# Seven of layer 1's eight MLP sets from seven block products, and GpSimd's taps of the second half from the first half's second product on, thirteen a block

## The chip, the cores and the metric

The kernel runs on one core of a Trainium2 chip. The metric is the device time of one execution in microseconds (us). The core has TensorE (PE, matrix products; PEld is its weight load), VectorE (DVE), ScalarE (ACT), GpSimd (POOL) and SyncE (SP, which issues most transfers). Each takes its instructions in program order from its own queue, and waits on semaphores for what another engine or a transfer has to deliver.

## The reference

1024 tokens of width 1024 pass two layers, all in float32. Layer 0 mixes tokens by a gated linear recurrence (HGRN2), layer 1 by a causal convolution; behind each stands an MLP with 4096 hidden columns and a squared ReLU, and each sum with the residual is normalised.

```python
u = h @ w_pw1 + b_pw1
a, gate = split(u, 2)
u = a * sigmoid(gate)
u = depthwise_conv(u, w_dw) + b_dw          # 31 taps, causal, each channel by itself
u = silu(layer_norm(u, ln_g, ln_b))
mix = u @ w_pw2 + b_pw2
x = layer_norm(ALPHA * x + mix, ...)
ff = square(relu(x @ ffn_w1[1])) @ ffn_w2[1]
x = layer_norm(ALPHA * x + ff, ...)
```

The change touches layer 1 from the convolution to the end of the MLP's first product.

## The kernel before

**Products.** Every float32 operand is cut into a high part (a cast on ScalarE) and a low part (a subtraction on VectorE, here called a cut), and a product is three matmuls: high by high, high by low, low by high. A matmul is 128 by 128 weights against 512 columns.

**Halves, blocks, sets.** The tokens are two halves of 512. The convolution's channels are eight blocks of 128. The MLP's 4096 hidden columns are eight sets of 512. A set can be done in two ways. Classical: eight products of 128 x 1024 by 1024 x 512, four for each half of the tokens (`UA`, first half; `UB`, second half), 96 matmuls a half. Or by the seven block products of a Strassen scheme (24 matmuls each, 168 in all): weights and tokens are cut into 2 x 2 blocks, sums of blocks (the forms) are multiplied, and sums of the seven results give the set. Products 1 and 2 need the first half of the tokens alone (`E`, function `soon`); products 3, 6, 5, 7 and 4 need the second half too (`L`, class `LateUp`). In the program's names `xa` and `xc` hold the tokens in high and low parts, and later forms of them; `xf` holds form 6; `s` is the scratch in which VectorE adds up a form; `wa` are weights for `UA`, `UB` and `E`; `raw`, `sum` and `fw` are weight blocks, their sums and their cut forms for `L` (class `LateForms`: four sums and five cuts for a set). `NEAR` is the number of sets done classically.

**The order of the stages** is the string `SEQ`. `P0j`, `P1j` are the pointwise products of channel block j for the two halves, `N` the normalisation of a half's convolution, `F` its activation, `S` the second pointwise product with the residual's normalisation, then `UA`, `E`, `UB`, `L` as above.

**The convolution** runs beside TensorE. The last `NPOOL[half]` of the 31 taps of a block go to GpSimd: ScalarE multiplies a tap (`prod`, L1555), GpSimd adds it to the sum `cb` (`cb<-cb,prod`; the first tap is written to `cb` directly, so 11 taps are 10 adds). The other taps are multiplied and added by VectorE in a PSUM bank (`ps<-u,par,ps`), the first by ScalarE (L1567). VectorE adds both, TensorE transposes the block (`ident,cb`), and ScalarE copies it (L1583) for `N`.

**What sets the order around the change.** A planner in the program (class `Background`) keeps clocks for TensorE, VectorE and GpSimd by costs of its own and places taps between the matmuls; `bg.hold` keeps GpSimd's taps back. Where a stage begins, `gate` ties the first tap to a tile of that stage: a one-element copy (L1550) that GpSimd has to make first. `bg.chores` are pieces of side work (the turning of normalised tokens, the forms) that are placed one by one between products; `bg.done()` places all that are left. The whole is then put in order once more by the framework's scheduler, which simulates a timeline and fixes each engine's queue before the program is built.

**S.** `second` normalises four tiles of 128 tokens, t = 0 to 3. VectorE makes mean and variance, GpSimd raises the variance to the power -1/2 (`mv<-mv,nhalf`, L518), ScalarE applies both (L1693), TensorE transposes (`ident,y`), ScalarE scales while it copies (L1667) and casts (L435), VectorE cuts.

**The forms of the second half** (`late_forms`): for two halves k of a block, the chores `fifth`, `sixth`, `fourth`, and, once nothing reads the plain tokens any more, `sevenths` and `last_form`, which write into `xc`.

**The loads of the MLP's second product** (`dh<-hf`) read tiles that `up_half` and `LateUp.form` have stored in device memory (`hf`, L1184). `ahead` lists weights that layer 0's free slots cut beforehand and store as `ready` (`spare`, L1398); there are 38 such tiles.

Of the kernel before, what the change touches and what calls it, by code (L numbers as in the profile page):

```python
# [17 lines left out]
S = 1024  # L18
KB = D // P
# [3 lines left out]
TAPS = 31  # L23
PAD = TAPS - 1
NFC = 8
NEAR = 2
ALPHA = 4.0 ** 0.25
LN_EPS = 1e-5
RMS_EPS = 1e-6
# [6 lines left out]

KBYTES = 220
PAIRS = [("q", 0), ("q", 1), ("q", 2), ("q", 3), ("g", 0), ("q", 4), ("q", 5), ("q", 6), ("g", 1), ("q", 7), ("g", 2), ("g", 3)]
NPOOL = (12, 11)
SEQ = "P00 P01 P02 P03 P04 P05 P06 P07 P10 P11 P12 P13 N0 P14 F0 P15 S0 P16 P17 UA0 UA1 E2 E3 N1 E4 F1 E5 E6 S1 E7 UB0 UB1 L2 L3 L4 L5 L6 L7"  # L40

# [225 lines left out]
def body(ctx, tc, d, out):  # L269
# [21 lines left out]
    def ring(kbs, shape, name, dt=F32):  # L291
        return Ring([view(kb, shape, dt, name) for kb in kbs])

    def run(kb, n, size):
        return [kb + i * size for i in range(n)]

    def slots(kbs, name):
        return ring(kbs, (2, 1024), name, F32R)

    def raws(kbs, name="raw"):  # L300
        return ring(kbs, (1024,), name)

    def bank(ids):
        return Ring([banks[:, i] for i in ids])

    class Room:


        def __init__(self, parts, want):
            self.rings = {}  # L310
            parts = [list(p) for p in parts]
            for name, (shape, n, *dt) in sorted(want.items(), key=lambda w: -prod(w[1][0])):
                kb, at = (prod(shape) + 7) // 8 / 32, []
                for _ in range(n):
                    part = next(p for p in parts if p[1] - p[0] >= kb)
                    at.append(part[0])
                    part[0] += kb
                self.rings[name] = ring(at, shape, name, *dt)
# [4 lines left out]
    bg = Background()  # L323
# [177 lines left out]
    for k in range(4):  # L501
        c = slice((k % 2) * HT, (k % 2 + 1) * HT)
# [608 lines left out]
    ha = [dram.tile([P, 2048], F32, name=f"ha{c}") for c in range(NFC)]  # L1111

    ready = {}
    ahead = [("wpw1", (j, i)) for j in range(KB) for i in (1, 0)] + [("wpw2", (n, k)) for n in range(2) for k in range(4)] + [("w1", (i,)) for i in range(4 * NEAR)] + [("w1q", (1, c, i)) for c in range(NEAR, NEAR + 3) for i in range(2)]

    def blocks(name, layer, c):
        return [d[name][layer, c, q] for q in range(4)]
# [133 lines left out]
    class LateUp(Up):  # L1251


        def __init__(self, xs):
            self.layer, self.xf, self.turned = 1, xs, NEAR
            self.zs, self.ws = bank((1, 5, 2, 6)), bank((3, 7, 0, 4))
            self.c = ring((132, 134, 136, 138, 128, 130), wide_t, "c")
            self.hr = ring((0, 8, 16, 24) if NEAR % 2 == 0 else (16, 24, 0, 8), (2, 2, HT), "hr")
            self.t = ring(run(112, 4, 2), (2, 256), "ht")
# [12 lines left out]
        def begin(self, c):  # L1272

            u = self.of[c]
            for q in range(2):
                u["z", q] = self.zs()
                nc.scalar.copy(out=u["z", q], in_=u["p"][:, q])
# [46 lines left out]
    def plan_down(layer, fw, fh):  # L1324
        fw.plan([form("w2", layer, c, i) for i in ORDER for c in range(NFC)])
        fh.plan([hf[layer][c][i] for i in ORDER for c in range(NFC)])
# [158 lines left out]
    wa = Slots(nc, vector, slots([192, 200, 208, 96, 104, 176], "wa"), raws(run(20, 3, 4)))  # L1485
    steps = [(w[:-1], int(w[-1])) for w in SEQ.split()]

# [27 lines left out]
    def pointwise(half, j):  # L1515
        wG, wA = wa.take(2)
        pg, pa = acc(), acc()
        product(pg, narrow(wG, x2T[half]))
        product(pa, narrow(wA, x2T[half]))
        wa.ahead(3)  # L1520
        if len(conv) >= 6:
            bg.flush(conv[-6])
        sg = big("r")
        nc.scalar.activation(sg, pg, AF.Sigmoid, bias=par[:, BPW1 + KB + j : BPW1 + KB + j + 1])
        u = big("u")
        if half == 0:
            nc.gpsimd.memset(u[:, :PAD], 0.0)
        else:
            nc.scalar.copy(out=u[:, :PAD], in_=halo[:, j, :])
        vector.scalar_tensor_tensor(out=u[:, PAD:], in0=pa, scalar=par[:, BPW1 + j : BPW1 + j + 1], in1=sg, op0=ALU.add, op1=ALU.mult)  # L1530
        if half == 0:
            nc.scalar.copy(out=halo[:, j, :], in_=u[:, HT:])
        sums = {}
        pooled.append(convolve_pool(half, j, u, sums))
        conv.append(convolve(half, j, u, sums, pooled[-1]))
        bg.pooled.append(pooled[-1])
        bg.jobs.append(conv[-1])

    def tap(j, i):
        return par[:, TAP + j * TAPS + i : TAP + j * TAPS + i + 1]  # L1540

    def convolve_pool(half, j, u, sums):
# [5 lines left out]
        if gate[0] is not None:  # L1548

            nc.gpsimd.tensor_copy(out=cb[:, :1], in_=gate[0])  # L1550
            gate[0] = None
        for k in range(TAPS - NPOOL[half], TAPS):
            first = k == TAPS - NPOOL[half]
            tp = cb if first else big("prod")
# [5 lines left out]
    def convolve(half, j, u, sums, other):  # L1560
# [6 lines left out]
        nc.scalar.activation(ca, u[:, :HT], AF.Identity, bias=par[:, BDW + j : BDW + j + 1], scale=tap(j, 0))  # L1567
        for i in range(1, TAPS - NPOOL[half]):
            if i == 6:
# [45 lines left out]
    def residual_of(half, y):  # L1615
        for t in range(NTB):
            nc.sync.dma_start(out=y[:, t, :], in_=kept[half][t])
        rest[half] = y
# [133 lines left out]
    for op, i in steps:  # L1752

        if op + str(i) in ("P10", "S0", "S1", "UA0", "UB0"):
            bg.done()

        bg.hold = op in ("N", "F", "S") or bg.hold and op == "P1"
        if op == "S":
            gate[:2] = sT[i][:, 1, KB - 1, :1].bitcast(F32), [ct[i][:, NTB - 1, :1]] * 2
            wa.behind = [gate[0]] * (3 if i == 0 else 0)  # L1760
        bg.margin = 12.0 if op == "S" else 5.0 if op in ("N", "F") else 0.0 if op != "P1" else bg.margin
        if op in ("P0", "P1"):
            pointwise(int(op[1]), i)
        elif op == "N":
            normalise(i)
        elif op == "F":
            finish(i)
        elif op == "S":
            second(i)
        elif op == "UA":  # L1770
            if i == 0:
                residual_of(1, view(32, (NTB, D), F32, "y"))
                for of in to_sum:
                    block_sums(*of, x3T[0][:2, 1, KB - 1, HT - 1 :].bitcast(F32), adds=adds)
            up_half(1, i, 0, wa, stA, x3T[0])
        elif op == "E":
            soon(i, wa, stA, {1: x3T[0][:, :, :4], 2: x3T[0][:, :, 4:]})
        elif op == "UB":
            if i == 0:
                wa.raws = None  # L1780
                wa.slots = slots((192, 200, 208, 96), "wa")
                stB = {"hr": ring(run(0, 2, 16), (8, 2, 256), "hb"), "r": ring(run(128, 2, 2), wide_t, "r"), "t": ring(run(112, 4, 4), (2, 2, 256), "ht")}
                xs, sevenths, last_form = late_forms()
            if i == NEAR - 1:
                bg.done()
                lf = LateForms(nc, vector, slots((104, 200, 208, 96, 192), "fw"), raws((176, 180, 184, 188)), raws((44,), "sum"))
                lf.todo = [[(blocks("w1q", 1, c),)] for c in range(NEAR, NFC)]
                lf.ahead(1)

                up = LateUp(xs)  # L1790
                up.bring(NEAR)

                def begin():
                    up.begin(NEAR)
                    for seventh in sevenths:
                        seventh()
                    last_form()

                up_half(1, i, 1, wa, stB, x3T[1], (lambda: None, lambda: lf.ahead(2), lambda: lf.ahead(3), begin))
            else:  # L1800
                up_half(1, i, 1, wa, stB, x3T[1])
        else:
            if i > NEAR:
                up.begin(i)
            if i < NFC - 1:
                up.bring(i + 1)
            for k in LATER if i > NEAR else (3, 6, 5, 7, 4):
                (f,) = lf.take(1)
                lf.ahead(3)
                up.form(i, k, f)  # L1810
                if i == NFC - 1 and k == 6:
                    fw = Slots(nc, vector, slots([48, 104, 200, 208, 144, 152, 160], "dw"), raws([40, 176, 180, 44, 140, 136], "dr"))
                    fh = Slots(nc, vector, slots([56, 32, 0, 8, 64, 72, 80], "dh"))
                    plan_down(1, fw, fh)
                if i == NFC - 1 and k in (6, 5):
                    fw.ahead(1 if k == 6 else 2)
                    fh.ahead(1 if k == 6 else 2)
# [106 lines left out]
```

## Time and profile before

| What | Value |
| --- | --- |
| Time, median of 3 runs | 2060.35 us (2057.59 to 2062.96) |
| Span of the profiled execution | 2068.3 us |
| TensorE busy | 2031.0 us, 98% |
| VectorE, ScalarE, GpSimd busy | 72%, 53%, 19% |
| Granted TensorE clock | 1.00 from 1301 to 1643 us |
| Product `S`, first half | 1306.8 to 1354 us |
| `P16`, `P17` | 1354 to 1379.8 us |
| `UA0` to `E6` with `N1`, `F1` | 1379.8 to 1483 us |
| `S`, second half | 1483 to 1531 us |
| `E7`, then `UB0`, `UB1` | 1531 to 1545, 1545 to 1588.7 us |
| `L2` to `L7` | from 1588.7 us |

The profiled execution is 8 us longer than the median of the runs; times on its axis are used for differences. A row of the timeline reads: start, duration, engine, line of the program, operation, what it writes and from what, shape, count; in brackets the idle time of the engine before it and what ended that. A row of the windows view reads: stretch, its length, then for each engine its busy time and its number of instructions, the granted clock, the transfers' share and rate.

### The profile page before, as it was taken

How to read it: one execution, taken by the hardware profiler on the slowest of the kernel's cores; microseconds unless marked ns; L12 is line 12 of the kernel's file. 1: busy time of each engine (PE TensorE's matmuls, PEld its weight loads, DVE VectorE, ACT ScalarE, POOL GpSimd, SP SyncE). 2: the span in 40 equal slices, each digit the busy share in tenths (PEclk: the TensorE clock that was granted, in tenths of full speed). 3: DMA queues.
4: the chain of work that ended last, by engine and by line, in shares of the span. 5: the costliest groups of instructions: out<-in, count | busy, mean ns of one | idle time of the engine just before them, and what ended most of it. 6: DMA issues, size and time to landing. Idle time of an engine off the chain costs nothing. (4 is left out here: it accounts for less than half of the span.)

```text
span 2068.3 us, 29719 instructions
## 1 busy us (share of the span) xinstructions
PE 2031.0 (98%) x11192; PEld 1674.5 (81%) x11192; DVE 1482.9 (72%) x1976; ACT 1090.2 (53%) x1727; POOL 388.4 (19%) x387
## 2 busy tenths in 40 slices
PE   8999999999999999999999999999999999999998
PEld 7888777788888888888888888888878878888886
DVE  8698877877775666565567898889589666755556
ACT  5456555641464555444444776488625555343333
POOL 0112222111001000000001699079210000100002
PEclk9999999999999999999999999999999999999999
DMA  4778889852689786999998855587759778996542
GB/s 186 224 195 233 238 224 270 254 189 81 187 288 298 243 295 221 353 341 332 335 349 292 309 193 185 190 323 271 256 215 339 245 232 291 386 292 204 193 155 102
DMA packets 183944, 517.55 MB, mean 250 GB/s; under 512 B 17912, under 2 KB 49784, under 8 KB 182776
## 3 DMA queue, kind: packets, MB, share of 16 engines
q1 hardware_dynamic: 168312, 456.93, 62.6%
q0 software_dynamic: 15488, 58.72, 12.3%
q8 instruction: 87, 1.43, 0.3%
q14 instruction: 57, 0.47, 0.1%
HBM read 380.85 MB, written 201.85 MB: 282 GB/s over the span
## 5 line engine op out<-in xcount | busy, mean ns | idle before, releaser
L204 PE MATMUL ps<-dw,dh 128*128 128x512 f32 x2688 | 611.6, 389 | 1.9 <-ACT dh L72 1.1
L204 PEld LDWEIGHTS ps<-dw,dh 128*128 128x128 f32 x2688 | 504.1, 188 | 107.2 <-ACT dh L72 1.6
L204 PE MATMUL ps<-x1f,fw 128*128 128x512 f32 x1344 | 309.3, 390 | 2.3 <-DVE c L204 1.2
L204 PEld LDWEIGHTS ps<-x1f,fw 128*128 128x128 f32 x1344 | 251.1, 188 | 56.2 <-ACT c L1224 2.3
L204 PE MATMUL ps<-xf,fs 128*128 128x512 f32 x1008 | 249.3, 398 | 4.1 <-issue 1.9
L204 POOL TENSOR_TENSOR cb<-cb,prod 128x512 f32<-128x512 f32 x168 | 222.7, 1334 | 12.9 <-ACT prod L1555 2.3
L204 DVE TENSOR_TENSOR dh<-dh 128x1024 fp32r<-128x1024 f32 x112 | 136.4, 1222 | 117.3 <-ACT dh L72 117.1
L204 PEld LDWEIGHTS ps<-xf,fs 128*128 128x128 f32 x1008 | 184.5, 189 | 43.4 <-issue 2.1
L204 DVE SCALAR_TENSOR_TENSOR ps<-u,par,ps 128x512 f32<-128x512 f32 x296 | 206.2, 750 | 11.0 <-ACT ps L1567 9.5
L72 ACT CAST dh<-dh 128x1024 fp32r<-128x1024 f32 x112 | 117.4, 1051 | 163.7 <-DMA dh<-hf 163.7
L204 PE MATMUL ps<-xa,wa 128*128 128x512 f32 x864 | 203.1, 392 | 0.1
L204 PEld LDWEIGHTS ps<-xa,wa 128*128 128x128 f32 x864 | 160.3, 188 | 33.3 <-ACT ha L1289 0.3
L204 DVE TENSOR_TENSOR dw<-dr,dw 128x1024 fp32r<-128x1024 f32 x112 | 136.2, 1222 | 66.6 <-ACT dw L72 65.9
L72 ACT CAST dw<-dr 128x1024 fp32r<-128x1024 f32 x112 | 117.0, 1051 | 119.2 <-PE ps L204 100.2
L1555 ACT ACTIVATE prod<-u,par 128x512 f32<-128x512 f32 x168 | 119.8, 726 | 36.6 <-POOL cb L204 35.7
L518 POOL TENSOR_TENSOR mv<-mv,nhalf 128x1 f32<-128x1 f32 x32 | 43.3, 1355 | 407.6 <-DVE mv L204 407.6
L1408 POOL COPY next<-ss 128x1 f32<-128x1 f32 x38 | 21.2, 558 | 413.8 <-DVE spare L204 265.1
L204 PE MATMUL ps<-xb,wa 128*128 128x512 f32 x384 | 91.1, 393 | 0.0
L204 PE MATMUL ps<-w,oT 128*128 128x512 f32 x384 | 89.5, 391 | 1.3 <-ACT oT L932 0.8
L204 DVE TENSOR_TENSOR spare<-next,spare 128x1024 fp32r<-128x1024 f32 x38 | 46.5, 1224 | 60.6 <-ACT spare L1401 60.5
L204 PE MATMUL ps<-vw,xf 128*128 128x512 f32 x336 | 79.8, 399 | 6.0 <-ACT vw L435 5.2
L204 PEld LDWEIGHTS ps<-w,oT 128*128 128x128 f32 x384 | 71.5, 188 | 16.6 <-ACT oT L932 1.2
(236 smaller groups left out, 2959.6 us busy)
## 6 DMA issues: line engine op xcount, KB each, us to landing
wa<-ready SPq DMA_DIRECT2D x140, 512.0 KB, 5.5
dh<-hf SPq DMA_DIRECT2D x112, 512.0 KB, 5.3
sum_w<-in_w_dram POOLq DMA_DIRECT2D x40, 1024.0 KB, 10.9
ready<-spare SPq DMA_DIRECT2D x76, 512.0 KB, 4.6
raw<-in_w1q_dram SPq DMA_DIRECT2D x66, 512.0 KB, 4.4
dr<-sum_w SPq DMA_DIRECT2D x64, 512.0 KB, 5.7
hf<-ht SPq DMA_DIRECT2D x112, 256.0 KB, 4.9
dr<-in_w_dram SPq DMA_DIRECT2D x48, 512.0 KB, 5.3
```

The source lines that it names most:

```text
L72: self.nc.scalar.copy(out=slot[:, 0, c], in_=raw[:, c])
L204: return op(*args, **kw)
L518: nc.gpsimd.tensor_tensor(out=dst, in0=src, in1=nhalf[:, :n], op=ALU.pow)
L1408: nc.gpsimd.tensor_copy(out=raw[:, :1], in_=now)
L1555: nc.scalar.activation(tp, u[:, k : k + HT], AF.Copy, scale=tap(j, k))
```

## The change

- `NEAR` goes from 2 to 1: set 1 is no longer `UA1` and `UB1`, but `E1` (products 1 and 2) and `L1` (3, 6, 5, 7, 4), seven block products.
- `NPOOL` goes from (12, 11) to (12, 13): GpSimd takes two more taps of each block in the second half, and VectorE two fewer.
- `bg.hold` no longer covers `S`: GpSimd's taps of the second half may start in the first half's `S`.
- `ahead` holds the same number of tiles: four classical weights fewer, and the block weights of two more sets.
- `bg.done()`, which places the remaining chores, moves from ahead of the last `UB` to its last product, since the last `UB` is now also the first.

```diff
-NEAR = 2
+NEAR = 1
-NPOOL = (12, 11)
-SEQ = "... S0 P16 P17 UA0 UA1 E2 E3 N1 E4 F1 E5 E6 S1 E7 UB0 UB1 L2 L3 L4 L5 L6 L7"
+NPOOL = (12, 13)
+SEQ = "... S0 P16 P17 UA0 E1 E2 E3 N1 E4 F1 E5 E6 S1 E7 UB0 L1 L2 L3 L4 L5 L6 L7"
-    ahead = ... + [("w1", (i,)) for i in range(4 * NEAR)] + [("w1q", (1, c, i)) for c in range(NEAR, NEAR + 3) for i in range(2)]
+    ahead = ... + [("w1", (i,)) for i in range(4 * NEAR)] + [("w1q", (1, c, i)) for c in range(NEAR, NEAR + 5) for i in range(2)]
     for op, i in steps:
         if op + str(i) in ("P10", "S0", "S1", "UA0", "UB0"):
             bg.done()
-        bg.hold = op in ("N", "F", "S") or bg.hold and op == "P1"
+        bg.hold = op in ("N", "F") or bg.hold and op == "P1"
...
             if i == NEAR - 1:
-                bg.done()
                 lf = LateForms(...)
                 lf.todo = [[(blocks("w1q", 1, c),)] for c in range(NEAR, NFC)]
                 lf.ahead(1)
                 up = LateUp(xs)
                 up.bring(NEAR)
                 def begin():
+                    bg.done()
                     up.begin(NEAR)
                     for seventh in sevenths:
                         seventh()
                     last_form()
```

What this does to the engines' queues is shown at three places. First GpSimd, from the end of the first half's taps (`mv<-mv,nhalf 128x4` is `N0`) through `S0` to `N1`; the single-column `mv` are `S0`'s roots.

```order
-L204 TENSOR_TENSOR cb<-cb,prod 128x512 x2
+L204 TENSOR_TENSOR cb<-cb,prod 128x512 x14
 L518 TENSOR_TENSOR mv<-mv,nhalf 128x1
-L204 TENSOR_TENSOR cb<-cb,prod 128x512 x68
+L204 TENSOR_TENSOR cb<-cb,prod 128x512 x4
+L518 TENSOR_TENSOR mv<-mv,nhalf 128x1
+L204 TENSOR_TENSOR cb<-cb,prod 128x512 x3
+L518 TENSOR_TENSOR mv<-mv,nhalf 128x1
+L204 TENSOR_TENSOR cb<-cb,prod 128x512 x3
+L518 TENSOR_TENSOR mv<-mv,nhalf 128x1
+L204 TENSOR_TENSOR cb<-cb,prod 128x512
+L86 COPY raw<-xa 128x1 x2
```

Before, three of `S0`'s four roots came first of all, then two adds, the fourth root and 68 adds. Now 14 adds stand ahead of the first root (the row that stays, L518), and the other three roots stand among the adds; 59 more adds follow, 84 in all.

Second, TensorE from the last products of the pointwise stage (`xb,wa`, to the end of `P17`) into `UA0` (`xa,wa`). Before:

```order
L204 MATMUL ps<-xb,wa 128x512 x9
L204 MATMUL ps<-ident,y 128x128 x4
L204 MATMUL ps<-xb,wa 128x512 x23
L204 MATMUL ps<-ident,y 128x128 x4
L204 MATMUL ps<-xb,wa 128x512 x5
L204 MATMUL ps<-ident,cb 128x128 x4
L204 MATMUL ps<-xb,wa 128x512 x5
L204 MATMUL ps<-xa,wa 128x512 x70
```

And now:

```order
L204 MATMUL ps<-xb,wa 128x512 x33
L204 MATMUL ps<-ident,y 128x128 x4
L204 MATMUL ps<-xb,wa 128x512 x2
L204 MATMUL ps<-ident,y 128x128 x4
L204 MATMUL ps<-xb,wa 128x512 x30
L204 MATMUL ps<-ident,y 128x128 x8
L204 MATMUL ps<-ident,cb 128x128 x8
L204 MATMUL ps<-xa,wa 128x512 x67
```

The transposes of the last token tile stood 33 and 10 matmuls ahead of `UA0`'s first; now all eight stand right ahead of it, and eight transposes of convolution blocks with them.

Third, the start of the `L` sets. TensorE's queue now, from `UB0` (`xc,wa`) on:

```order
L204 MATMUL ps<-xc,wa 128x512 x22
L204 MATMUL ps<-xc,fw 128x512 x8
L204 MATMUL ps<-xf_12586,fw 128x512 x6
L204 MATMUL ps<-xa,fw 128x512 x6
L204 MATMUL ps<-xf_12586,fw 128x512 x6
L204 MATMUL ps<-xa,fw 128x512 x18
L204 MATMUL ps<-xf_12586,fw 128x512 x36
L204 MATMUL ps<-xa,fw 128x512 x24
L204 MATMUL ps<-xc,fw 128x512 x48
```

Ahead of these rows `UB0` and product 3 of set 1 are mixed; 120 matmuls lie before the first that reads `xf`, where there were 216. The last row holds product 3 of set 2 and then product 7 of set 1. In the same stretch VectorE's queue, where form 7 is cut into `xc`:

```order
L204 TENSOR_TENSOR s<-xc 128x1024
L204 TENSOR_TENSOR xc<-s,xc 128x1024
L204 TENSOR_TENSOR s<-s,xc 128x1024
L204 TENSOR_TENSOR dh<-dh 128x1024
L204 TENSOR_TENSOR s<-s,xc 128x1024
L204 TENSOR_TENSOR xc<-s,xc 128x1024
```

Between the cut of the last plain tokens and the second of these cuts there were 41 operations; now there are 52, and the first `dh` stands between the two cuts, on ScalarE between the two casts as well.

More of the change, by code (lines that the diff above doesn't have):

```diff
@@ L38 @@
 PAIRS = [("q", 0), ("q", 1), ("q", 2), ("q", 3), ("g", 0), ("q", 4), ("q", 5), ("q", 6), ("g", 1), ("q", 7), ("g", 2), ("g", 3)]
-NPOOL = (12, 11)
-SEQ = "P00 P01 P02 P03 P04 P05 P06 P07 P10 P11 P12 P13 N0 P14 F0 P15 S0 P16 P17 UA0 UA1 E2 E3 N1 E4 F1 E5 E6 S1 E7 UB0 UB1 L2 L3 L4 L5 L6 L7"
+NPOOL = (12, 13)
+SEQ = "P00 P01 P02 P03 P04 P05 P06 P07 P10 P11 P12 P13 N0 P14 F0 P15 S0 P16 P17 UA0 E1 E2 E3 N1 E4 F1 E5 E6 S1 E7 UB0 L1 L2 L3 L4 L5 L6 L7"
 ORDER = (1, 2, 6, 5, 7, 3, 4)
@@ L1113, in body @@
     ready = {}
-    ahead = [("wpw1", (j, i)) for j in range(KB) for i in (1, 0)] + [("wpw2", (n, k)) for n in range(2) for k in range(4)] + [("w1", (i,)) for i in range(4 * NEAR)] + [("w1q", (1, c, i)) for c in range(NEAR, NEAR + 3) for i in range(2)]
+    ahead = [("wpw1", (j, i)) for j in range(KB) for i in (1, 0)] + [("wpw2", (n, k)) for n in range(2) for k in range(4)] + [("w1", (i,)) for i in range(4 * NEAR)] + [("w1q", (1, c, i)) for c in range(NEAR, NEAR + 5) for i in range(2)]
     def blocks(name, layer, c):
```

## The prediction

> **What bounds the kernel now.** I read the page first, for the bounding engine.
>
> ```profile
> span 2068.3 us, 29719 instructions
> PE 2031.0 (98%) x11192; PEld 1674.5 (81%) x11192; DVE 1482.9 (72%) x1976; ACT 1090.2 (53%) x1727; POOL 388.4 (19%) x387
> PEclk9999999999999999999999999999999999999999
> L204 POOL TENSOR_TENSOR cb<-cb,prod 128x512 f32<-128x512 f32 x168 | 222.7, 1334 | 12.9 <-ACT prod L1555 2.3
> L1555 ACT ACTIVATE prod<-u,par 128x512 f32<-128x512 f32 x168 | 119.8, 726 | 36.6 <-POOL cb L204 35.7
> ```
>
> TensorE is busy for 98% of the span at full granted clock. Time therefore comes in two ways only: fewer matmuls, or a changed wait of TensorE. The averages of the other engines say nothing about waits, so next I cut the touched stretch into its stages.
>
> ```profile
> core 0: us, PE busy (x) PEld busy (x) DVE busy (x) ACT busy (x) POOL busy (x), PEclk, DMA share, GB/s
> 1301.00:1354.00 53.00, 52.38 (x248) 42.88 (x247) 48.02 (x83) 25.76 (x42) 1.62 (x3) 1.00 0.52 194
> 1354.00:1380.00 26.00, 26.00 (x131) 21.53 (x130) 20.58 (x32) 25.46 (x54) 22.47 (x21) 1.00 0.97 364
> 1380.00:1458.00 78.00, 78.00 (x353) 64.55 (x352) 75.45 (x108) 63.82 (x103) 74.08 (x55) 1.00 0.76 279
> 1545.00:1589.00 44.00, 44.00 (x197) 36.46 (x196) 41.38 (x38) 20.69 (x31) 0.00 (x0) 1.00 0.93 330
> 1589.00:1616.00 27.00, 27.00 (x121) 22.36 (x120) 23.64 (x24) 17.14 (x24) 0.00 (x0) 1.00 0.86 294
> ```
>
> S0 (first half's second product, 1301 to 1354) leaves GpSimd idle. P16 and P17 follow up to 1380, with ScalarE full (25.46 of 26). Then UA0 to E6, with VectorE and GpSimd both nearly full. At 1545 UB0 and UB1 cover 44 us in which VectorE works 41.4: it is making the block forms that the late sets multiply. TensorE never waits in these rows, but behind it are helpers with 3 us or less of room. The timeline of TensorE shows the points where it takes their results:
>
> ```profile
> 1376.59 0.60 PE L204 MATMUL ps<-ident,y 128*128 128x128 f32 x4
> 1378.19 0.60 PE L204 MATMUL ps<-ident,cb 128*128 128x128 f32 x4
> 1379.79 16.04 PE L204 MATMUL ps<-xa,wa 128*128 128x512 f32 x70
> 1468.57 0.60 PE L204 MATMUL ps<-ident,cb 128*128 128x128 f32 x4
> 1477.91 1.04 PE L204 MATMUL ps<-ident,y 128*128 128x128 f32 x8
> 1545.08 43.78 PE L204 MATMUL ps<-xc,wa 128*128 128x512 f32 x192
> 1588.70 5.60 PE L204 MATMUL ps<-xc,fw 128*128 128x512 f32 x24
> 1594.14 5.60 PE L204 MATMUL ps<-xf,fw 128*128 128x512 f32 x24
> 1605.02 5.60 PE L204 MATMUL ps<-xc,fw 128*128 128x512 f32 x24
> ```
>
> From 1545.08 to 1588.70 are 192 matmuls: 0.227 us each. I call 1545.08, the start of UB0, T0.
>
> **Part 1: the matmuls saved.** UA1 and UB1 were 96 matmuls each. E1 (two block products of 24) and L1 (five) are 48 and 120. So 24 matmuls go, -5.5 us, 48 fewer ahead of S1 and 24 more behind it. The weight forms that set 1 now needs are staged or made on VectorE, which only matters where VectorE is late, below.
>
> **Part 2: GpSimd's taps begin in S0.** The rows of the helpers around S0:
>
> ```profile
> 1324.47 0.69 DVE L204 TENSOR_TENSOR xa<-z,xa 128x512 fp32r<-128x512 f32 x1
> 1340.78 0.54 POOL L518 TENSOR_TENSOR mv<-mv,nhalf 128x1 f32<-128x1 f32 x1 [44.23 <-DVE mv L204]
> 1341.55 1.25 ACT L1693 ACTIVATE y<-y,mv 128x1024 f32<-128x1024 f32 x1 [5.00 <-DVE mv L204]
> 1355.37 2.67 POOL L204 TENSOR_TENSOR cb<-cb,prod 128x512 f32<-128x512 f32 x2 [0.48 <-ACT cb L1555]
> 1357.99 0.55 POOL L518 TENSOR_TENSOR mv<-mv,nhalf 128x1 f32<-128x1 f32 x1
> 1359.85 1.25 ACT L1693 ACTIVATE y<-y,mv 128x1024 f32<-128x1024 f32 x1 [0.17 <-DVE mv L204]
> 1367.43 45.04 POOL L204 TENSOR_TENSOR cb<-cb,prod 128x512 f32<-128x512 f32 x32 [1.01 <-ACT prod L1555]
> 1377.99 1.55 ACT L1667 ACTIVATE x<-ps,sm 128x128 f32<-128x128 f32 x4
> 1381.68 0.69 ACT L435 CAST xa<-x 128x512 fp32r<-128x512 f32 x1
> 1439.41 18.85 POOL L204 TENSOR_TENSOR cb<-cb,prod 128x512 f32<-128x512 f32 x12
> ```
>
> The gate of the taps opens with the last cut of xa, 1325.2; the first product and add are through ScalarE and on GpSimd by about 1328. In the new order 14 adds stand ahead of the first of S0's four reciprocal roots (mv, L518), then 4, 3 and 3 between them. An add costs 45.04/32 = 1.41 us. So the first root goes from 1340.8 to 1328.3 + 14 x 1.41 + 0.5 = 1348.6, and the fourth to 1328.3 + 24 x 1.41 + 4 x 0.54 + some 6 for copies and for prods that ScalarE delivers late = about 1370, not 1358.0. Behind the fourth root come, in a chain, the normalisation on ScalarE (L1693), 8 transposes, 8 turning activations (L1667), two casts and two cuts. Today that takes from 1357.99 to the last cast's end at 1382.4, 24 us, because these actions stand among prods on a full ScalarE and among matmuls. Moved together, the shortest I can add up is about 19 us: 1389 to 1390 for the last piece, and 1382.4 + 12 = 1394 if the whole shift goes through.
>
> Who waits: TensorE. In the old order the last transposes (1376.59) stand with 10 matmuls behind them before UA0, and UA0 begins at 1379.79 with no wait. In the new order the last 8 transposes and then 8 of cb stand right ahead of UA0's first matmul, in one queue, so all of P17 is spent and nothing else covers the chain. UA0 begins at about 1390.5: a stall of **10.7** (bounds 2.5, if ScalarE's prods move into its free half of S0, 25.76 of 53, and leave room for the turns; 14, the whole shift).
>
> **Part 3: the end of the taps.** 84 adds instead of 70 (twelve a block over seven blocks; block 8 was done before). Before they took 1355.37 to 1458.26, 1.47 each with all waits; 84 x 1.47 from 1328.3 is 1452, with the four roots and copies 1455, and up to 1459 where ScalarE starves them between 1354 and 1390. The last transposes of cb need that and VectorE's add behind it. Counted by matmuls in the new order, they come 67 us after UA0's start (286 matmuls and the transposes between), where the old order had 88.8 (1379.79 to 1468.57). So UA0 plus 67 has to be no earlier than 1452 to 1460: if UA0 starts on time, TensorE waits 5 to 13 there; if it starts at 1390.5, it arrives at 1457.5 and waits 0 to 2.5. The two stalls are one budget: **12 us together, 5 to 14**. The 16 taps that VectorE loses (two a block, 0.66 of pitch each, 10.6) gain nothing, as GpSimd ends last. The 48 matmuls fewer (10.9) are thus spent: T0 is about where it was.
>
> A rule of the Trainium skill speaks against this part: SBUF — State Buffer, "Who interferes with whom", says that a VectorE instruction with two SBUF inputs contends with a GpSimd instruction that reads SBUF. The trace bears it out, in this row against 1.22 for the same form elsewhere; by it S0's two-input operations would stretch too.
>
> ```profile
> 1453.64 2.10 DVE L204 TENSOR_TENSOR wa<-raw,wa 128x1024 fp32r<-128x1024 f32 x1 [0.52 <-ACT wa L72]
> ```
>
> VectorE's cut here takes 2.10 beside GpSimd's adds. S0 has some 16 such half-width operations (y<-y,b_pw and xa<-x,xa) that were alone and now run beside adds; at half of 0.88 more each that is up to 7 us on an engine with 5 free in S0 (48.02 of 53). I take none of it into the sum, and give it a rival.
>
> **Part 4: L1 needs the second half's forms 22 us earlier.**
>
> ```profile
> 1547.56 0.69 DVE L204 TENSOR_TENSOR xc<-ps,xc 128x512 fp32r<-128x512 f32 x1
> 1577.52 1.23 DVE L204 TENSOR_TENSOR xf<-s,xf 128x1024 fp32r<-128x1024 f32 x1
> 1598.76 1.22 DVE L204 TENSOR_TENSOR xc<-s,xc 128x1024 fp32r<-128x1024 f32 x1
> 1585.55 0.32 SPq L1184 DMA_DIRECT2D hf<-hb  x1
> 1588.47 0.32 SPq L90 DMA_DIRECT2D dh<-hf  x1
> 1594.20 1.06 ACT L72 CAST dh<-dh 128x1024 fp32r<-128x1024 f32 x1 [1.28 <-DMA dh<-hf]
> ```
>
> VectorE cuts the last piece of x at T0 + 2.5, the second half of xf (product 6) at T0 + 32.4 after 23 operations of 1.135 us pitch and 3.3 us of waits, and the second of xc (product 7) at T0 + 53.7. TensorE wanted them at T0 + 49 (first piece of xf) and T0 + 60, so there was room. Now 120 matmuls (27.2 us) lie before xf and 156 (35.4) before its second half, and in VectorE's new order 32 operations, not 23, stand before that half's cut, since set 1's weights stand among them: T0 + 2.5 + 0.6 + 32 x 1.135 + 3.3 + 1.2 to its end = T0 + 44. TensorE waits up to 8.5 there; less, to 5, if weight operations that wait for loads are quicker. Then xc: the scheduler put set 2's products 6, 5 and 3 ahead, so its second half is wanted 252 matmuls on, T0 + 57.1. VectorE is there after 52 operations (47 full, 5 half wide): T0 + 3.1 + 56.3 + 3.3 + 1.2 = T0 + 64, 7 late, which the first wait has covered.
>
> But ahead of that last cut both ScalarE and VectorE now stand at the cast and cut of a dh tile whose store comes from L1 itself, at about T0 + 52 plus what TensorE has waited. Store to load was 2.9 us here (1585.55 to 1588.47), load to cast 5.7: with the cast, the xc cast and two operations behind them the cut ends at T0 + 66 to 69, 9 to 12 late. I take **10.5**, and **2.5** for the next set, whose weights VectorE makes with 23.64 of 27 us already taken there (0 to 5). Together **13**, bounds 7 (dh in time, next set clean) and 19. From about T0 + 100 the stages are TensorE's own again; it gives nothing back.
>
> **The sum.** -5.5 + 12 + 13 = +19.5 us. It is made against the profiled execution's span, 2068.3, which is 8 us above the median of the runs; the difference goes onto the median: 2060.35 + 19.5 = **2080 us**. Bounds: -5.5 + 5 + 7 = +6.5 (2067) and -5.5 + 14 + 19 = +27.5 (2088).
>
> **The rivals.**
> - *All covered.* ScalarE's tap products fit into S0's idle half, the roots come in time, GpSimd ends by 1450, and the forms find room: only the 24 matmuls show, 2054.9. For it speaks that TensorE waits nowhere now; against it that VectorE had 2.6 of 44 us free where it is to be 22 us earlier. Beyond that it would need both windows. Chance 0.15.
> - *One of two.* The taps are covered to 1 us and only L1 stalls: -5.5 + 1 + 13 = +8.5, 2069; or L1's forms come by and only the taps stall: -5.5 + 12 = +6.5, 2067. Chance 0.17.
> - *Contention (more than forecast).* S0's VectorE operations stretch by the 7 us above: the fourth root and UA0 5 later, 2085 to 2092. It decides from the point where VectorE's S0 work passes its 53 us. Chance 0.10.
> - My forecast, 2073 to 2088: 0.58.
>
> **Numbers.** A change under 0.3% (6.2 us) cannot be told from none, so faster is below 2054.2 and slower above 2066.5. All covered lies on the lower border: 0.08 faster, 0.07 same; one of two gives 0.04 more to same. With a little for what I don't see, 0.09 faster, 0.12 same, 0.79 slower. The range reaches from the near side of the rivals to the far: 2058 to 2091.
>
> **What would show it.** In the changed kernel's timeline: UA0's first matmul behind a wait for an xa cut or for ScalarE's copies, near 1390; the four roots near 1349 to 1370; the adds' end near 1455; waits before xf's second half (5 to 8) and before xc (2 to 5), with the dh cast waiting for its load. I am wrong if UA0 starts within 2 us of 1380 and the last cb transposes wait nothing, or if TensorE runs from UB0 to set 3 with under 3 us of waits.

## The result and the profile after

The changed kernel takes 2082.94 us (median of 4 runs, 2079.85 to 2086.63), the kernel before 2058.97 in the same comparison: 1.0122 times as long, 95% interval 1.0109 to 1.0136, so 24 us slower. The profiled execution has a span of 2078.1 us. Up to the end of the first half's `S` the program is nearly the same, and the time at which that point is reached scatters from profile to profile (1354.2 us before, 1347.6 in `before_thin` below, whose edit lies behind it); so I compare from there on. `S`'s last product ends at 1354.23 before and at 1341.31 after (with the eight transposes that now follow it); from there to the end are 714.1 and 736.8 us, 22.7 more.

TensorE's timeline after, around `UA0` and at the end of the convolution (start, duration, then the instruction, its count, and in brackets the wait before it and what ended it):

```profile
1366.34 0.66 PE L204 MATMUL ps<-ident,y 128*128 128x128 f32 x4 [0.69 <-ACT x L1667]
1373.26 1.08 PE L204 MATMUL ps<-ident,cb 128*128 128x128 f32 x4 [6.26 <-POOL cb L204]
1375.22 1.12 PE L204 MATMUL ps<-ident,cb 128*128 128x128 f32 x4 [0.88 <-ACT x L1667]
1375.99 2.06 PE L204 MATMUL ps<-xa,wa 128*128 128x512 f32 x4
1378.33 15.73 PE L204 MATMUL ps<-xa,wa 128*128 128x512 f32 x63 [0.29 <-DVE xa L204]
...
1445.47 0.60 PE L204 MATMUL ps<-ident,cb 128*128 128x128 f32 x4
1445.82 10.96 PE L204 MATMUL ps<-xa,wa 128*128 128x512 f32 x47
1456.62 1.04 PE L204 MATMUL ps<-ident,y 128*128 128x128 f32 x8
```

`UA0` begins 34.7 us after `S`'s end, where it was 25.6: 9.1 us later, in one place, 7.8 us of it waits and the rest transposes at a lower clock (last section). The last transposes of the blocks and the normalisation behind them wait for nothing. The profile names GpSimd for the long wait; the other engines' rows show who it is:

```profile
1312.02 0.18 POOL L1550 COPY cb<-xa 128x1 f32<-128x1 f32 x1 [27.60 <-DVE xa L204]
1333.09 0.56 POOL L518 TENSOR_TENSOR mv<-mv,nhalf 128x1 f32<-128x1 f32 x1
1350.34 1.00 POOL L518 TENSOR_TENSOR mv<-mv,nhalf 128x1 f32<-128x1 f32 x1
1425.89 14.52 POOL L204 TENSOR_TENSOR cb<-cb,prod 128x512 f32<-128x512 f32 x10 [0.32 <-ACT prod L1555]
1367.32 0.69 ACT L435 CAST xa<-x 128x512 fp32r<-128x512 f32 x1
1371.65 1.51 ACT L1667 ACTIVATE x<-ps,sm 128x128 f32<-128x128 f32 x4 [1.24 <-DVE xa L204]
1373.65 1.51 ACT L1667 ACTIVATE x<-ps,sm 128x128 f32<-128x128 f32 x4
1377.86 0.65 ACT L435 CAST xa<-x 128x512 fp32r<-128x512 f32 x1
1362.92 6.01 DVE L204 SCALAR_TENSOR_TENSOR ps<-u,par,ps 128x512 f32<-128x512 f32 x9
1370.82 0.73 DVE L204 TENSOR_TENSOR xa<-x,xa 128x512 fp32r<-128x512 f32 x1
```

The two groups of block transposes start 0.1 us after the two turning activations end (1373.16 and 1375.16), so I read both waits as waits for ScalarE to leave a PSUM bank, as the profile itself has it for the second. The first activation waits for a buffer that VectorE's cut at 1370.82 frees, and that cut's cast was done at 1368.0 while VectorE was in a row of nine taps. It is the turning chain of the last two token tiles, on two full engines: of the 35 us from 1341 on, VectorE is busy for 34.97 and ScalarE for 32.44.

Then the start of the `L` sets; `T0`, the start of `UB0`, is 1530.41 here:

```profile
1530.41 16.65 PE L204 MATMUL ps<-xc,wa 128*128 128x512 f32 x72 [0.29 <-ACT xc L1045]
...
1572.89 7.11 PE L204 MATMUL ps<-xf,fw 128*128 128x512 f32 x30 [1.14 <-DVE xf L204]
...
1594.36 0.73 PE L204 MATMUL ps<-xc,fw 128*128 128x512 f32 x2 [3.20 <-ACT xc L435]
1595.62 6.89 PE L204 MATMUL ps<-xc,fw 128*128 128x512 f32 x22 [0.53 <-DVE xc L204]
1602.34 5.60 PE L204 MATMUL ps<-xa,fw 128*128 128x512 f32 x24
...
1622.04 1.19 PE L204 MATMUL ps<-xf,fw 128*128 128x512 f32 x4 [3.02 <-ACT fw L72]
1626.48 6.42 PE L204 MATMUL ps<-xf,fw 128*128 128x512 f32 x20 [0.90 <-DVE fw L204]
1637.27 11.04 PE L204 MATMUL ps<-xc,fw 128*128 128x512 f32 x48
```

From `T0` to 1602.34 stand 264 matmuls, 59.9 us at 0.2267, in 71.9 us: 12.1 late. From there to 1637.27 are 120, 27.2 us, in 34.9: 7.7 late. After that TensorE runs as before. VectorE is busy for 60.1 of the first 65 us, and the two cuts that TensorE waited for stand late in its queue (first two windows, where VectorE's busy time is the third after the length; then rows of VectorE):

```profile
1530.00:1560.00 30.00, 28.75 (x127) 23.29 (x126) 27.54 (x25) 15.22 (x23) 0.00 (x0) 1.00 0.71 254
1560.00:1595.00 35.00, 28.49 (x119) 21.41 (x117) 32.52 (x32) 15.43 (x20) 0.00 (x0) 1.00 0.61 202
...
1571.61 1.22 DVE L204 TENSOR_TENSOR xf<-s,xf 128x1024 fp32r<-128x1024 f32 x1
1590.87 1.23 DVE L204 TENSOR_TENSOR dh<-dh 128x1024 fp32r<-128x1024 f32 x1 [1.12 <-ACT dh L72]
1594.34 1.23 DVE L204 TENSOR_TENSOR xc<-s,xc 128x1024 fp32r<-128x1024 f32 x1 [1.11 <-ACT xc L435]
```

For all runs I read three lengths from TensorE's timeline: A, from the last matmul of `S` to the first of `UA0`; B, from there to the first of `UB0`; C, from there to the first of the MLP's second product. The 24 matmuls saved are 48 fewer in B (-10.9 us) and 24 more in C (+5.4). In A 0.8 us is not wait where eight transposes now follow `S` that stood inside it.

| Kernel | A | B | C | time / before, 95% interval |
| --- | --- | --- | --- | --- |
| before | 25.6 | 165.3 | 204.2 | 1 |
| changed | 35.5 | 154.4 | 229.0 | 1.0122 (1.0109 to 1.0136) |
| set1_alone | 25.6 | 160.9 | 230.4 | 1.0088 (1.0057 to 1.0119) |
| taps_alone | 35.5 | 165.2 | 204.9 | 1.0029 (1.0014 to 1.0045) |
| hold_13 | 24.6 | 180.4 | 231.2 | 1.0186 (1.0159 to 1.0213) |
| dh_late | 35.4 | 154.3 | 228.2 | 1.0085 (1.0059 to 1.0111) |
| thin_forms | 35.3 | 153.3 | 212.8 | 1.0022 (1.0009 to 1.0036) |
| before_thin | 25.6 | 165.5 | 205.6 | 0.9992 (0.9978 to 1.0007) |
| thin_weights | 35.4 | 154.5 | 217.5 | 1.0042 (1.0026 to 1.0058) |
| thin_both_dh | 35.4 | 153.9 | 214.6 | 1.0034 (1.0017 to 1.0050) |
| pool_sums | 35.5 | 153.6 | 229.4 | 1.0104 (1.0079 to 1.0129) |
| no_prod | 25.4 | 152.2 | 228.2 | 1.0125 (1.0096 to 1.0154) |
| hold_10_thin | 25.6 | 165.0 | 213.1 | 1.0022 (1.0009 to 1.0035) |

Other chips ran these kernels, and their runs of the kernel before spread more (2055 to 2070), so the ratios are good to about 0.2 to 0.3%. What lies ahead of A and behind C varies by several us from run to run (the stretch behind C between 315 and 321 us). Where an edit does not reach it, a length repeats within 1.5 us, and the readings below rest on these lengths.

### The profile page after: what moved, and what is told of

Same layout as the page of the kernel before. It is cut to its first block, busy times and chain, and to the rows that moved or that the text cites. A ratio compares the mean times of both kernels' runs of the same rounds, so it can differ in the third digit from the quotient of the medians.

```text
span 2078.1 us, 29720 instructions
## 1 busy us (share of the span) xinstructions
PE 2031.2 (98%) x11168; PEld 1672.6 (80%) x11168; DVE 1489.3 (72%) x1975; ACT 1107.3 (53%) x1754; POOL 405.7 (20%) x402
## 4 chain that ended last, share of the span: by engine, by line
PE 71%; DMA 12%; DVE 10%; issue 3%; ACT 2%; SPq 1%; POOL 1%; DVEq 0%; POOLq 0%; ACTq 0%
PE ps L204 71%; DMA sum_w<-in_w_dram 5%; DVE ps L204 2%; DMA raw<-in_w1q_dram 1%; DMA dr<-in_w_dram 1%; DMA dh<-hf 1%; DVE fw L204 1%; DVE y L204 1%; DVE qk L204 1%; DMA hf<-hr 1%; DVE xf L204 1%; DMA vr<-in_wv_dram 0%; DVE vr L204 0%; DVE xa L204 0%; DVE ht L204 0%
## 5 line engine op out<-in xcount | busy, mean ns | idle before, releaser
L204 POOL TENSOR_TENSOR cb<-cb,prod 128x512 f32<-128x512 f32 x184 | 241.4, 1320 | 18.6 <-ACT prod L1555 7.3
L204 DVE SCALAR_TENSOR_TENSOR ps<-u,par,ps 128x512 f32<-128x512 f32 x280 | 194.6, 747 | 10.1 <-ACT ps L1567 8.7
L204 PE MATMUL ps<-xa,wa 128*128 128x512 f32 x816 | 195.1, 396 | 0.3 <-DVE xa L204 0.3
L204 PEld LDWEIGHTS ps<-xa,wa 128*128 128x128 f32 x816 | 152.5, 190 | 32.2 <-DVE xa L204 1.2
L1555 ACT ACTIVATE prod<-u,par 128x512 f32<-128x512 f32 x184 | 131.7, 728 | 43.4 <-POOL cb L204 42.6
L518 POOL TENSOR_TENSOR mv<-mv,nhalf 128x1 f32<-128x1 f32 x32 | 42.7, 1336 | 359.0 <-DVE mv L204 355.7
L1198 ACT ACTIVATE c<-c 128x512 f32<-128x512 f32 x76 | 47.2, 627 | 75.3 <-DVE c L204 75.1
```

Source lines behind the costliest of these rows:

```text
L204: return op(*args, **kw)
L518: nc.gpsimd.tensor_tensor(out=dst, in0=src, in1=nhalf[:, :n], op=ALU.pow)
L1198: nc.scalar.activation(t, src, AF.Relu, scale=scale)
L1555: nc.scalar.activation(tp, u[:, k : k + HT], AF.Copy, scale=tap(j, k))
```

## The experiments

**1. Each part of the change alone.** `set1_alone`:

```diff
-        bg.hold = op in ("N", "F") or bg.hold and op == "P1"
+        bg.hold = op in ("N", "F", "S") or bg.hold and op == "P1"
-NPOOL = (12, 13)
+NPOOL = (12, 11)
```

> Only set 1's move to block products (E1, L1); GpSimd's taps are held back in the first half's S and are eleven a block, as before. By the theory (two separate stalls: GpSimd's early taps delay UA0, VectorE is late in L1) UA0 starts without a wait, the taps end where they did while TensorE arrives 11 us earlier, so about 6 us of wait stand at the end of the convolution, and the wait of about 19 us between UB0 and set 3 stays: -5.5 + 6 + 19 = +19 to +20 us against the kernel before, only 3 us less than the changed kernel. By the rival, that the early taps are the one cause, almost all of the loss goes: -5 to 0 us against the kernel before.

2083.29 against 2061.68 us: 21.6 slower by the medians, 18 by the ratio. A is back, B is 6.5 longer than the 154.4 that the matmuls leave, C has 20.8 beyond its matmuls. The waits in B stand in the normalisation behind the last transposes:

```profile
1457.21 4.38 PE L204 MATMUL ps<-xa,wa 128*128 128x512 f32 x18
1463.64 1.36 PE L204 MATMUL ps<-ident,y 128*128 128x128 f32 x8 [2.06 <-ACT y L1613]
1468.49 1.12 PE L204 MATMUL ps<-ident,y 128*128 128x128 f32 x4 [3.50 <-ACT z L1634]
```

`taps_alone`:

```diff
 # the kernel before, with
-NPOOL = (12, 11)
+NPOOL = (12, 13)
-        bg.hold = op in ("N", "F", "S") or bg.hold and op == "P1"
+        bg.hold = op in ("N", "F") or bg.hold and op == "P1"
```

> Only GpSimd's taps: no hold in the first half's S, thirteen a block; set 1 stays classical. By the theory UA0 starts 9 us late, as in the changed kernel, nothing later gives it back and nothing later is added: +9 us against the kernel before. By the rival, that UA1's 48 additional matmuls and the earlier end of the taps give the time back, 0 to +3 us.

2068.82 against 2061.68 us, +6 by the ratio (interval +3 to +9); A is 9.9 longer as in the changed kernel, B and C are as before; 3.7 us less behind C, within its spread, make the ratio smaller. So the two parts cost separately: the taps their 9 us in A, set 1 its 20 us in C, and the taps take 6.5 us out of B that set 1 alone would have there.

**2. Hold the taps, but keep thirteen.** `hold_13`:

```diff
-        bg.hold = op in ("N", "F") or bg.hold and op == "P1"
+        bg.hold = op in ("N", "F", "S") or bg.hold and op == "P1"
```

> The changed kernel with GpSimd's taps held back in the first half's S again, still thirteen a block. By the theory the wait at UA0 (9 us) goes, but 84 adds of 1.47 us begin only at the end of S: they end about 126 us after it, TensorE reaches the last transposes of the blocks 113 us after it, so 13 us of wait there, and the normalisation behind them, with nothing to cover it, 10 us more: +15 us against the changed kernel, some +39 against the kernel before. By the rival, that the hold costs nothing since TensorE has other work, -9 us against the changed kernel, +14 against the kernel before.

2103.06 us, 1.0186 times before. A loses its wait and B gains 26.0:

```profile
1475.82 1.12 PE L204 MATMUL ps<-ident,cb 128*128 128x128 f32 x4 [13.01 <-DVE cb L204]
1482.81 1.97 PE L204 MATMUL ps<-ident,y 128*128 128x128 f32 x8 [5.87 <-ACT y L1613]
1487.66 1.12 PE L204 MATMUL ps<-ident,y 128*128 128x128 f32 x4 [2.89 <-ACT z L1634]
```

13.0 us at the last block, as worked out from 84 adds of 1.47 us, and 8.8 in the normalisation, where 10 were expected; the rest of the 26 is a slower TensorE behind the waits (last section). With thirteen taps a block on GpSimd the early start is needed.

**3. What makes `UA0` wait.** `no_prod` (the second half's GpSimd taps are added without their weights):

```diff
-            tp = cb if first else big("prod")
-            nc.scalar.activation(tp, u[:, k : k + HT], AF.Copy, scale=tap(j, k))
+            if half == 1 and not first:
+                tp = u[:, k : k + HT]
+            else:
+                tp = cb if first else big("prod")
+                nc.scalar.activation(tp, u[:, k : k + HT], AF.Copy, scale=tap(j, k))
```

> The changed kernel without ScalarE's multiplications of the second half's taps on GpSimd: GpSimd adds the shifted inputs themselves (these taps then have weight 1, the output is another). 91 ScalarE operations of 0.73 us go, GpSimd's adds stay as many and stand ahead of S's roots as before, 15, 4, 3 and 2; the scheduler then puts the last transposes 20 matmuls ahead of UA0. It splits the 9 us at UA0 between its two candidates. If the roots behind the adds carry it (5 us late in the changed kernel), 4 to 5 us of wait at UA0 stay; if ScalarE, full of products between the turning activations, carries it, 1 us or less stays, with roots as late as they were. From UB0 on nothing changes: +10 to +20 us against the kernel before in all.

Its time, 2086.82 against 2059.13 us, says nothing on this place: the new order also made TensorE wait some 12 us at the first half's normalisation, ahead of `S`, so the 10 to 20 us forecast were missed. A does:

```profile
1371.71 0.55 POOL L518 TENSOR_TENSOR mv<-mv,nhalf 128x1 f32<-128x1 f32 x1 [1.23 <-DVE mv L204]
1383.40 1.18 ACT L435 CAST xa<-x 128x512 fp32r<-128x512 f32 x2
1385.92 0.94 PE L204 MATMUL ps<-xa,wa 128*128 128x512 f32 x3
1387.08 8.24 PE L204 MATMUL ps<-xa,wa 128*128 128x512 f32 x35 [0.21 <-DVE xa L204]
```

The fourth root is later than in the changed kernel (11.1 us after `S`'s end at 1360.6, there 9.0, before 3.8), and still `UA0` waits 0.2 us. From that root to the last cast's end are 12.9 us here, 28.2 in the changed kernel and 24.4 before. So without ScalarE's products the chain is short enough to cover a root that late. It does not follow that the late root costs nothing in the changed kernel, since products stood in this chain before too (16, now 18). Against `S`'s end the last cast ends 9.0 us later than before: 5.2 us because the root is later, 3.8 because the chain is longer. That is what `UA0` waits for.

What makes the chain 3.8 us longer is not separated. In `no_prod` the scheduler's order differs too (the last transposes stand 20 matmuls earlier), and GpSimd stands idle for 14.8 us in this stretch, where in the changed kernel it adds all the while and most of VectorE's cuts beside it take 1.09 to 1.64 us in place of 0.68 (before, two of them did, with 1.12 and 1.17).

**4. What L1 waits for.** `thin_forms` leaves out 12 of the 20 additions in the second half's forms: those of low parts, so the forms lose precision, and their loads, casts and cuts stay.

```diff
             vector.scalar_tensor_tensor(out=o, in0=p, scalar=-1.0, in1=part(t, 0, k), op0=ALU.mult, op1=ALU.subtract)
-            less(o, o, part(t, 1, k))
...
             less(o, part(t, 0, k1), part(u, 0, k2))
-            vector.tensor_tensor(out=o, in0=o, in1=part(t, 1, k1), op=ALU.add)
-            less(o, o, part(u, 1, k2))
```

> The changed kernel with 12 of VectorE's 20 additions of the second half's forms left out (the forms then hold wrong values); casts, cuts, weights and loads stay. That is 12 x 1.135 = 13.6 us of VectorE less between the end of S and form 7. By the theory, that VectorE is late by the number of its operations, the waits before xf and xc go and those before set 3 stay: -10 to -13 us against the changed kernel, +11 to +14 against the kernel before. By the rival, that loads of weights and of dh set the pace, 0 to -3 us.

C falls by 16.2 us, more than forecast: of 19.4 us beyond the matmuls 3.1 stay. 3.4 us of the fall is the clock, which is not lowered anywhere in this C (last section). The time is 2068.63 against 2064.14 us. `before_thin` is the control, the same edit in the kernel before:

> The kernel before with the same 12 additions of form pieces left out as in thin_forms. By the theory VectorE has room there (TensorE has 44 us of UB0 and UB1 over it), so 13.6 us of VectorE less change nothing: 0 us, within 2. If the edit itself makes the kernel faster in some other way (fewer reads, another order of TensorE's work), it would show here too, -5 us or more, and thin_forms would not speak for VectorE being late.

0.9992, no change, and C is 1.4 longer if anything. The edit helps only where VectorE is late.

`thin_weights` takes VectorE's sums of weight blocks from the first two late sets (their products are wrong):

```diff
+        self.units = getattr(self, "units", 0) + 1
+        if self.units <= 2:
+            for x in (a[1], a[0], a[2], a[0], a[3]) if first else (a[0], a[2], a[1], a[0], a[3]):
+                self.form(x)
+                yield
+            return
         self.add(a[0], a[2], a[0])
```

> The changed kernel with the four sums of weight blocks of the first two late sets left out (their products are wrong); cuts, casts and loads stay, as do all forms of the tokens. That is 8 x 1.135 = 9.1 us of VectorE less, 4.5 of it ahead of xf's second half. By the theory -5 to -9 us against the changed kernel; by the rival that loads set the pace, 0 to -2 us.

C falls by 11.5 us, again more than the 9.1 us of VectorE taken away. What goes are the waits up to product 7; the wait before set 3 stays, as long as it was:

```profile
1612.79 2.07 PE L210 MATMUL ps<-xf,fw 128*128 128x512 f32 x4 [3.14 <-ACT fw L72]
```

So that one is not a wait for VectorE's backlog. In the changed kernel, too, VectorE is by then waiting for others, and the sum of weight blocks that set 3 needs waits for its load (SPq is SyncE's queue):

```profile
1600.03 0.69 DVE L204 TENSOR_TENSOR c<-c,ps 128x512 f32<-128x512 f32 x1 [4.47 <-PE ps L204]
1614.09 0.62 SPq L173 DMA_DIRECT2D raw<-in_w1q_dram  x1
1619.46 1.23 DVE L204 TENSOR_TENSOR sum<-raw 128x1024 f32<-128x1024 f32 x1 [0.78 <-DMA raw<-in_w1q_dram]
1620.95 1.03 ACT L72 CAST fw<-sum 128x1024 fp32r<-128x1024 f32 x1
```

TensorE goes on at 1622.04, when that cast has ended. The rival, that loads set the pace, is wrong for the waits up to product 7 and right for the last step of this one. In `thin_forms` this wait is 1.0 us, with other orders in the queues; why the load is issued so late in the others, no run separates.

`thin_both_dh` joins both with the next edit, in which the `dh` tiles use their slots in another order:

> The changed kernel with both left out, 12 additions of forms and 8 sums of weights, and the dh load kept from standing ahead. By the theory nothing of VectorE's is late from UB0 on: -17 to -20 us against the changed kernel, which leaves the 9 us at UA0 less the 5.5 of the 24 matmuls: +3 to +6 against the kernel before. If 8 us or more of waits remain between UB0 and set 4, the cause there is another than VectorE's work.

C falls by 14.4 us, short of the forecast. Between `UB0` and the fourth late set nothing is left: from `T0` at 1538.57 to 1636.65 stand 432 matmuls, 97.9 us of work in 98.1. What remains comes later, and the other order of the slots brought it:

```profile
1742.88 10.49 PE L210 MATMUL ps<-xc,fw 128*128 128x512 f32 x38 [2.90 <-ACT c L1230]
```

**5. The dh tile by itself.** `dh_late`:

```diff
-    fh = Slots(nc, vector, slots([56, 32, 0, 8, 64, 72, 80], "dh"))
+    fh = Slots(nc, vector, slots([56, 0, 8, 64, 72, 80, 32], "dh"))
```

> The changed kernel with the slots of the dh tiles in another order, so that the first dh load cannot be put ahead of the last set any more; ScalarE's cast and VectorE's cut of dh then do not stand before form 7's second cut. By the theory that cut comes 4 us earlier and the wait in front of it goes: -4 us against the changed kernel (+20 against the kernel before). By the rival that only the number of VectorE's operations counts (one of 1.14 us less), -1 us. If the transfers were what L1 waits for, more than -8 us.

The length C is 0.8 us shorter. The ratio is lower by 7.6 us (1.0085, where the changed kernel has 1.0122; the intervals just meet), which none of the three lengths shows; since the two were measured on different chips, I go by the lengths. The place itself did what was forecast: product 7's end comes 68.0 us after `T0` (1534.96), not 71.9, 3.9 earlier.

```profile
1596.55 0.73 PE L204 MATMUL ps<-xc,fw 128*128 128x512 f32 x2 [0.98 <-ACT xc L435]
1602.94 5.60 PE L204 MATMUL ps<-xa,fw 128*128 128x512 f32 x24
1623.33 1.39 PE L204 MATMUL ps<-xf,fw 128*128 128x512 f32 x4 [3.64 <-ACT fw L72]
1752.85 10.50 PE L204 MATMUL ps<-xc,fw 128*128 128x512 f32 x38 [2.62 <-ACT c L1224]
```

Half a microsecond of it goes into a longer wait for set 3's weights, and the rest into a new wait at the last set, 1752.85, like that of `thin_both_dh`. So the early `dh` costs 3.9 us where it stands, and this way of moving it gives them away again.

**6. The sums on the idle engine.** `pool_sums` has GpSimd add set 1's weight blocks; values are unchanged:

```diff
+        own = self.vector
+        if first:
+            self.vector = self.nc.gpsimd
         self.add(a[0], a[2], a[0])
         s = self.add(a[0], a[3])
+        if first:
+            x1 = self.add(a[1], s, a[1])
+            x2 = self.add(a[2], a[3], a[2])
+            self.vector = own
```

> The changed kernel with set 1's four sums of weight blocks on GpSimd, which is idle there, instead of VectorE; the values are the same. By the count of VectorE's operations -4.5 us against the changed kernel. By the rule that a VectorE operation with two inputs from SBUF and a GpSimd operation that reads SBUF shut each other out (SBUF - State Buffer, Who interferes with whom, in the Trainium skill), VectorE's operations beside the four adds go from 1.22 to some 2.1 us, as one cut beside GpSimd's taps did: what the count gives is lost again, -1 to +3 us.

C is 0.4 us longer. GpSimd's and VectorE's rows of the same 13 us:

```profile
1543.79 3.27 POOL L127 TENSOR_TENSOR sum<-raw 128x1024 f32<-128x1024 f32 x1
1544.83 3.32 DVE L215 SCALAR_TENSOR_TENSOR s<-s,xc 128x1024 f32<-128x1024 f32 x1
1554.74 1.21 DVE L215 TENSOR_TENSOR s<-s,xc 128x1024 f32<-128x1024 f32 x1
```

As long as GpSimd adds, VectorE finishes one operation for each of GpSimd's: 3.3 to 3.4 us in place of 1.21. Its queue ahead of the second half of `xf` is 7 operations shorter, the four that moved and three that the new order puts later, which saves 7 x 1.14 = 8.0 us; the four stretched operations cost 4 x 2.1 = 8.4. So C shows nothing of the move. The Trainium skill (SBUF — State Buffer, "Who interferes with whom") states this exclusion, and this run agrees.

**7. The parts together, made small.** `hold_10_thin` is `thin_forms` with this:

```diff
-        bg.hold = op in ("N", "F") or bg.hold and op == "P1"
+        bg.hold = op in ("N", "F", "S") or bg.hold and op == "P1"
-NPOOL = (12, 13)
+NPOOL = (12, 10)
```

> Set 1 in block products with each known wait made as small as a variant can: taps held back in S, ten a block (VectorE takes 21), and the 12 additions of form pieces left out as in thin_forms. By the theory the parts add: -5.5 for the matmuls, 0 at UA0, 6 at the end of the convolution (the normalisation's chain behind the last transposes has 18 matmuls over it, whatever the taps), 3 from UB0 on: +3 to +5 us against the kernel before. By the rival that GpSimd's taps make the wait at the convolution's end, eight adds a block fewer take it away: -2 us or less against the kernel before.

2064.72 against 2059.13 us, +4.5 by the ratio. That this lies in the forecast range is partly luck: the three lengths add up to +8.6, and the stretches around them were shorter in this profile. A is 25.6, C has 3.5 beyond its matmuls, but B has 10.6, not 6, with 5.92 and 2.89 us of wait in the normalisation. Eight adds fewer on GpSimd did not help, so GpSimd does not set that wait: the taps have gone to VectorE, and the chain of the normalisation has nothing over it. No variant here is faster than the kernel before.

## Why the prediction was right, step by step

The time forecast was 2080 us, the measured one 2082.9, and both places of loss were the forecast ones. Inside the terms, errors cancel. The terms:

- **Part 1**, -5.5: as the matmul counts and B and C have it.
- **Part 2**, 10.7 us at `UA0`: 9.1. The sum was near, its split was not. The first root was to come 5.6 us ahead of `S`'s end and came 8.2 ahead, the fourth 15.8 behind it and came 9.0 behind. The gate opened where it was forecast, 29 us ahead of `S`'s end; but the first add started 28.3 us ahead, not 25.9, and from the first root to the fourth GpSimd waited 2.3 us for ScalarE's products and `S`'s variances, where some 6 had been allowed. The chain behind the fourth root was to take 19 us and took 28. Two errors of some 7 to 9 us, of opposite sign: that the sum came near is luck. What `UA0` feels is the difference from before, 5.2 us of root and 3.8 of chain (experiment 3).
- **Part 3**, 1.3 us more at the convolution's end (12 in all with part 2): none. The 84 adds ended at 1440.4, 5 us ahead of the last transposes. Nor are the two stalls one budget, as the prediction had it: in `no_prod` `UA0` starts with 0.2 us of wait and the block transposes wait for nothing. Taps that are held do move the wait there (26 us with thirteen, 6.5 with eleven), but not all of it is GpSimd's: experiment 7 has the wait with ten taps, in the normalisation's chain.
- **Part 4**, 13 us: 19.4 (12.1 + 7.7, less what was there before). Up to product 7 it held: the second half of `xf` was to be ready at `T0` + 44 and was at `T0` + 42.4, `xc` at 66 to 69 and was at 65.2, 10.5 us late in all against 12.1, and `thin_forms` and `thin_weights` both take these waits away. The `dh` tile was worth 3.9 of it, as forecast. The term mis-sized is the 2.5 us (0 to 5) for the next set's weights: 7.7. Its reason, a VectorE that is full there, fails as well: from 1595 to 1620 us VectorE is busy for 14.6 of 25 us, and the wait ends with the chain of load, sum and cast in experiment 4. Why that load comes late stays open.
- **What the sum left out** is the clock (last section): 1.7 us behind each of two waits in C, inside the 12.1 and the 7.7, and 2.3 us behind the wait at `UA0`.
- **Rivals.** "All covered" and "one of two" fell with A and C. Contention in `S` did not decide: VectorE's two-input operations did stretch (two `y<-y,b_pw` at 1319.35 took 3.38 us together), but the roots came sooner than forecast. In `pool_sums` it decides.

## What to carry to other kernels

Matmuls that are saved were also the cover of other engines' work: before taking 5 us from TensorE, count the operations of the engine that has to be ready earlier, up to the last operand that it delivers and one stage beyond. Work that is moved to an idle engine stands ahead of that engine's small operations: 24 adds ahead of `S`'s fourth root made it 5.2 us later, with nothing over the chain behind it. An idle engine whose operations stretch the busy one's is no help: look at the busy one's durations beside it first.

## What the hardware showed that I had not expected

TensorE comes out of a wait of about 3 us at a lower granted clock. The windows of the changed kernel around the two waits ahead of product 7 and of set 3, cut where the clock changes, with 3.41 us and twice that ahead of the first change (the first number after the length is TensorE's busy time, the column before the transfers' share is the granted clock):

```profile
1588.98:1592.40 3.42, 2.18 (x10) 1.48 (x8) 2.30 (x3) 1.05 (x1) 0.00 (x0) 1.00 0.21 81
1592.40:1595.81 3.41, 0.93 (x3) 0.49 (x4) 2.05 (x2) 1.04 (x1) 0.00 (x0) 1.00 0.00 0
1595.81:1599.22 3.41, 3.41 (x9) 2.63 (x9) 0.00 (x0) 0.00 (x0) 0.00 (x0) 0.50 0.54 157
1599.22:1602.63 3.41, 3.41 (x17) 2.79 (x16) 0.78 (x2) 1.81 (x4) 0.00 (x0) 1.00 0.01 1
...
1623.12:1629.95 6.83, 5.65 (x13) 3.98 (x13) 6.83 (x9) 2.32 (x4) 0.00 (x0) 0.50 1.05 370
```

Ahead of the program's end the half clock comes in stretches of 3.41 us or a multiple of it (10.24 at `UA0`). In the 3.41 us ahead of these drops TensorE was busy for 0.93 us, 1.08 (from 1619.71), none (from 1367.13) and, in `dh_late`, 1.01 (from 1750.45); behind 2.18 us the clock stayed. Where between 1.08 and 2.18 the limit lies, these rows do not show.

The 22 matmuls at 1595.62 took 6.89 us and the 20 at 1626.48 took 6.42, where 22 x 0.2267 + 0.16 is 5.15 and 20 give 4.70: 1.7 us lost behind each of the two waits. Behind the wait at `UA0` the first 67 matmuls lost 2.3 us in the same way. In `dh_late` a wait of 2.62 us was enough: the 38 matmuls at 1752.85 took 10.50 us, not 8.8. The Trainium skill (TensorE: Matmul & The Clock Gate, "Part 1: The HAM clock gate (the "warmup" mystery)") says that the array falls to half its clock after an idle window of about 3.4 us and comes back after a busy one of the same length; these waits are a little shorter than that and the clock fell all the same. The kernel before pays nothing of this in the stretch compared here; in layer 0 it does twice, at half the clock from 272.6 to 276.0 us and from 392.1 to 395.5, at waits of 4.86 and 2.27 us. A stall of about 3 us here costs its length and some 1.7 us more, the longer one at `UA0` 2.3 behind it.
